# Two more seven-product pairs per half and three DMA-made low parts, in the three projections to the model width

## The chip, the cores and the metric

One core of a Trainium2 chip runs the whole program. The metric is the device time of one execution in microseconds; for one core that is the time of this core. PE is the matrix engine (TensorE), DVE the vector engine (VectorE), ACT the scalar engine (ScalarE), POOL is GpSimd, SP is the engine that issues the loads (SyncE). HBM is the memory outside the core, SBUF the working memory inside it, and PSUM the eight accumulator banks that PE writes.

## The reference

The reference computes two layers of an encoder on 256 positions of width 2048, all in float32. Each layer is a token mixer and a gated feed-forward network (FFN), each followed by a layer norm with a scaled residual:

```python
for i in range(DEPTH):                      # DEPTH = 2
    m = gmlp_mixer(...) if i % 2 == 0 else mla_mixer(...)
    x = layer_norm(ALPHA * x + m, ...)
    f = conv_ffn(x, ...)
    x = layer_norm(ALPHA * x + f, ...)
```

The first mixer ends in `(u * s) @ w_out` with w_out of 6144 x 2048; each FFN ends in `(silu(g) * a) @ w_down` with w_down of 5504 x 2048. These three products, of 48, 43 and 43 row blocks of 128, are the "projections to the model width" that the change touches. Their left operands have 256 rows.

## The kernel before, in words

**Products of split numbers.** PE multiplies numbers of a shortened float32 (float32r). To keep the precision, each operand is cut into a high part (the number rounded to float32r) and a low part (the number minus its high part), and a product is three matmuls: high x high, low x high, high x low (`prod_b`, lines 280 to 286). The left operand is held on chip; the weights come from HBM once and are cut on chip. ACT makes the high part of a chunk of weights (line 104, a copy with rounding), DVE the low one (line 105, a subtraction).

**The feed.** All weights of the program, in the order of their use, are one list of chunks of 128 x 2048 numbers, 1 MB each; `Feed` (lines 66 to 143) loads them on SP's queue (`_load`, line 80 or 85), cuts them (`_split`) and hands them out (`next`). When chunk i is handed out, the cutting of chunks i+1 and i+2 and the loading of two more have been written into the program. All these tiles (raw, high `wh`, low `wl`, and others) share one pool of 22 buffers of 8 KB per partition with the operands that live longer (line 152). A tile takes a buffer over when the last reader of the tile before it is done, so a load can be held up by PE, DVE or ACT. The engines run their own instructions strictly in the order in which they were written.

**A pair of row blocks.** In a projection a chunk holds two consecutive row blocks k, k+1 of the weights for one half of the 2048 columns. The plain way to multiply them with the two blocks of 128 positions is `Banks.eight` (line 337): two position blocks x two column groups of 512 x two k, eight products of 128 x 128 by 128 x 512, 24 matmuls. The other way is `Banks.seven` (line 344), Strassen's scheme in Winograd's form: seven products, 21 matmuls, of sums of the operands. The sums of the weights are made by `Feed._seven` (line 115): DVE adds 1024, 512 and 512 columns (`ts`), then ACT and DVE cut the plain quarters that are needed (`wh`, `wl`, 1536 columns) and the sums (`th`, `tl`, 1536 and 512 columns). The sums of the left operand are made by `combine` (line 206): four DVE operations of 128 x 128, one ACT cast and one DVE subtraction of 128 x 512; they are made once and used in both halves (`Sums.make`, line 396). A seven-product pair takes five buffers of the pool beside its raw chunk. Its four further accumulators are PSUM banks of their own (`OWN`, line 324); after the last such pair of a half `rest` (line 354) adds them up on ACT and DVE and `fold` adds the results to the residual.

**A projection.** `down` (line 405) runs the left half of the columns, then the right half, over the pairs in the order of `halves(n_k)` (line 53): the left half in ascending order, the right half in an order of "quads" of four row blocks. `BACK_SEVEN` (line 63) lists the first row block of the five pairs per half that go by seven products: 4, 10, 18, 24, 32. The last three pairs of the right half are kept back for the start of the layer norm. Left operands are cut quad by quad as they are needed (`quad`, line 384) and dropped after their last use.

The chunk kinds are "seven", "wide" (cut in one piece) and "" (cut in two pieces); `back` (line 174) sets them for the projections.

Of the kernel before, what the change touches and what calls it, by code (L numbers as in the profile page):

```python
# [12 lines left out]
ALU = mybir.AluOpType  # L13
# [36 lines left out]
V_SEVEN = [()] + [(2, 3, 4)] * 5  # L50


def halves(n_k):


    one = [tuple(range(k, min(k + 2, n_k))) for k in range(0, n_k, 2)]
    n = (n_k + 3) // 4
    quads = [n - 1, 1, 2, 0, 4, 3, 6, 8, 5, 7] + list(range(9, n - 1))
    return [one, [u for q in quads for u in one[2 * q : 2 * q + 2]]]

BACK_SEVEN = (4, 10, 18, 24, 32)


class Feed:
# [24 lines left out]
    def _split(self):  # L91
        i = self.split
        cols, kind = self.chunks[i][1:]
        raw = self.raw.pop(i)
        if kind == "seven":
            self.parts[i] = self._seven(i, raw)
            self.split += 1
            return
        hi = self.pool.tile([P, 2048], F32R, tag="big", name=f"wh{i}")
        lo = self.pool.tile([P, 2048], F32R, tag="big", name=f"wl{i}")  # L100
        step = 512 if i == 0 else cols if kind == "wide" and i > 2 else 1024 if cols == 2048 else cols // 2
        for o in range(0, cols, step):
            c = slice(o, o + step)
            self.nc.scalar.copy(hi[:, c], raw[:, c])  # L104
            self.nc.vector.tensor_tensor(lo[:, c], raw[:, c], hi[:, c].bitcast(F32), ALU.subtract)  # L105
            if i == 0 and o == step:
                self.between[1]()
        self.parts[i] = (hi, lo)
        self.split += 1
# [20 lines left out]

    def ahead(self, n_load, n_split):
        while self.split < min(n_split, len(self.chunks)):
            if self.loaded == self.split:
                self._load()
            self._split()
        while self.loaded < min(n_load, len(self.chunks)):
            self._load()
# [9 lines left out]
def trunk(ctx: ExitStack, tc: tile.TileContext, x, xT, gm_in, gm_wout, ffn_up, ffn_dn,  # L147
# [19 lines left out]
    chunks = []  # L167
# [6 lines left out]
    def back(w, n_k):  # L174

        for hf, units in enumerate(halves(n_k)):
            c = slice(hf * 1024, (hf + 1) * 1024)
            for u in units:
                if len(u) == 1:
                    chunks.append((w[u[0], :, c], 1024, "wide"))  # L180
                else:
                    chunks.append((w[u[0] : u[0] + 2, :, c].rearrange("k p c -> p k c"), 2048,
                                   "seven" if u[0] in BACK_SEVEN else "wide"))

    back(gm_wout, NF_GM)
    chunks += [(ffn_up[0, i], 2048, "") for i in range(n_up)]
    back(ffn_dn[0], NF_FF)
    chunks += [(ml_q[i], 2048, "") for i in range(4)]
    chunks += [(ml_kv[i], 3 * KVR, "") for i in range(5)] + [(ml_kv[5, :, 0:KVR], KVR, "")]
    chunks += [(ml_b[i], 2048, "") for i in range(ml_b.shape[0])]  # L190
    chunks += [(ml_out[i], 2048, "") for i in range(ml_out.shape[0])]
    chunks += [(ffn_up[1, i], 2048, "") for i in range(n_up)]
    back(ffn_dn[1], NF_FF)


# [209 lines left out]
    def down(n_k, src, tag, ln, sums, skew=SKEW):  # L405
# [3 lines left out]
        quads = sums.quads  # L409
        late = []  # L410
        for hf, units in enumerate(halves(n_k)):
            n = len(units)
            last = [u for u in units if u[0] in BACK_SEVEN][-1]


            acc = Banks(f"{tag}{hf}", OWN + DIRECT if hf else DIRECT + OWN)
            for i, u in enumerate(units):
                left = n - 1 - i if hf == 1 else n
                for u2 in units[i : i + 3]:
                    sums.quad(u2[0] // 4, n_k)  # L420
                if i + 1 < n and units[i + 1][0] in BACK_SEVEN:
                    sums.make(units[i + 1][0])
# [5 lines left out]
                if left < skew:  # L428
                    late.append((a, *got))
                elif u[0] in BACK_SEVEN:  # L430
                    acc.seven(a, sums.got[u[0]], *got)
# [246 lines left out]
    for gi in range(12):  # L678
        acc = [bank(f"u{gi}_{f}") for f in range(4)]
        for c in range(4):  # L680
            hi, lo = feed.next()
# [5 lines left out]
        if gi == 10:  # L687
            for k in BACK_SEVEN[:2]:
                sums.make(k)
# [17 lines left out]
    def ffn(layer, ln, acc, end, last):  # L707
# [27 lines left out]
        for gi in range(1, 22):  # L735
# [13 lines left out]
            if gi == 20:  # L749
                for k in BACK_SEVEN[:2]:  # L750
                    sums.make(k)
# [66 lines left out]
    for c in range(6):  # L818
        hi, lo = feed.next()
        for j in range(3 if c < 5 else 1):  # L820
            k = 3 * c + j
# [31 lines left out]
    for c in range(2):  # L853
        hi, lo = feed.next()
        for j in range(2):
            k = 2 * c + j
# [107 lines left out]
    for hf in range(2):  # L964
        acc = [[bank(f"vv{hf}_{b}_{f}") for f in range(2)] for b in range(2)]
        for c in range(2):
            hi, lo = feed.next()
            for j in range(2):

                k = 2 * c + j  # L970
# [7 lines left out]
        for b in range(2):  # L978
            for f in range(2):
                c = slice(hf * 1024 + f * 512, hf * 1024 + (f + 1) * 512)  # L980
# [7 lines left out]
    for t in range(3, H + LAG):  # L988
        k = t - LAG
        if k >= 0:  # L990
            if k % 2 == 0:
                hi, lo = feed.next()
            w = slice((k % 2) * 1024, (k % 2) * 1024 + 1024)
# [21 lines left out]
    for c in range(8):  # L1015
        left = 7 - c
        hi, lo = feed.next(splits=2 if left > 5 else 3 if left > 2 else 4, loads=2 if left > 2 else 1)
        for j in range(2):
            k = 2 * c + j
            w = slice(j * 1024, (j + 1) * 1024)  # L1020
# [104 lines left out]
```

## Time and profile before

| what | value |
|---|---|
| time, median of 3 runs | 2501.7 us (2501.2 to 2503.17) |
| the profiled execution | 2504.94 us, its span 2503.2 us |
| granted clock of PE, mean | 0.997 |
| first projection (gMLP), about | 552 to 800 us of the span |
| second (FFN of layer 0), about | 1293 to 1512 us |
| third (FFN of layer 1), about | 2266 to 2490 us |
| read from HBM, written | 476.00 MB, 2.10 MB |

The profile's page gives the busy time of each engine over the span, then the chain of work that ended last, followed back from the last instruction, and groups of equal instructions with count, busy time and mean duration; other views show the same instructions by stretch of time, by line or in order. A row such as `L105 DVE TENSOR_TENSOR wl<-raw,wh` is the instruction of line 105 that writes tile wl from raw and wh; buffer numbers are left out, so one row stands for many chunks. Matmuls are pipelined: the pitch between two is shorter than the duration of one. In the rows of stretches the columns are: stretch, its length, then the busy time and number of instructions of PE, PE's weight loads, DVE, ACT and POOL, then the granted clock, the share of the DMA queues and GB/s.

### The profile page before, as it was taken

How to read it: one execution, taken by the hardware profiler on the slowest of the kernel's cores; microseconds unless marked ns; L12 is line 12 of the kernel's file. 1: busy time of each engine (PE TensorE's matmuls, PEld its weight loads, DVE VectorE, ACT ScalarE, POOL GpSimd, SP SyncE). 2: the span in 40 equal slices, each digit the busy share in tenths (PEclk: the TensorE clock that was granted, in tenths of full speed). 3: DMA queues.
4: the chain of work that ended last, by engine and by line, in shares of the span. 5: the costliest groups of instructions: out<-in, count | busy, mean ns of one | idle time of the engine just before them, and what ended most of it. 6: DMA issues, size and time to landing. Idle time of an engine off the chain costs nothing.

```text
span 2503.2 us, 32484 instructions
## 1 busy us (share of the span) xinstructions
PE 2484.7 (99%) x13066; PEld 2138.5 (85%) x13066; DVE 1840.0 (74%) x2439; ACT 1335.0 (53%) x1763; POOL 2.9 (0%) x17
## 2 busy tenths in 40 slices
PE   9999999999999999999999999999999999999998
PEld 7888888888887888888888888988888888888886
DVE  6887866678787767666778887756686676668796
ACT  6565644445464546545655564565365555546553
POOL 0000000000000000000000000000000000000000
PEclk9999999999999999999999999999999999999999
DMA  7555554556566555555546674444555455555654
GB/s 276 214 190 202 202 177 161 184 192 204 187 207 252 188 182 202 185 180 176 195 156 202 217 269 157 156 143 178 183 205 183 165 206 178 182 180 172 214 203 168
DMA packets 86310, 480.19 MB, mean 192 GB/s; under 512 B 7696, under 2 KB 8336, under 8 KB 46608
## 3 DMA queue, kind: packets, MB, share of 16 engines
q1 hardware_dynamic: 86160, 478.13, 54.2%
q8 instruction: 102, 1.67, 0.3%
q14 instruction: 48, 0.39, 0.0%
HBM read 476.00 MB, written 2.10 MB: 191 GB/s over the span
## 4 chain that ended last, share of the span: by engine, by line
PE 98%; DVE 1%; ACT 0%; DMA 0%; issue 0%; SPq 0%; DVEq 0%; ACTq 0%
PE up L164 36%; PE u L164 11%; PE dn_q L164 9%; PE dn_p L164 6%; PE v_q L164 5%; PE wo_q L164 5%; PE v_p L164 3%; PE mo L164 3%; PE dn_e L164 3%; PE wo_p L164 3%; PE wo_e L164 2%; PE upf L164 2%; PE v_e L164 2%; PE mkv L164 1%; PE qn L164 1%; PE kn L164 1%
## 5 line engine op out<-in xcount | busy, mean ns | idle before, releaser
L105 DVE TENSOR_TENSOR wl<-raw,wh 128x1024 fp32r<-128x1024 f32 (+3 forms) x664 | 929.3, 1424 | 218.7 <-ACT wh L104 161.4
L104 ACT CAST wh<-raw 128x1024 fp32r<-128x1024 f32 (+3 forms) x664 | 786.4, 1215 | 341.1 <-DVE wl L105 125.2
L164 PE MATMUL up<-xhl,wh 128*128 128x512 f32 x2624 | 610.7, 390 | 0.0
L164 PEld LDWEIGHTS up<-xhl,wh 128*128 128x128 f32 x2624 | 487.4, 188 | 97.7
L164 PEld LDWEIGHTS up<-xhl,wl 128*128 128x128 f32 x2624 | 325.8, 192 | 6.4
L164 PE MATMUL up<-xhl,wl 128*128 128x256 f32 x2624 | 328.1, 283 | 0.0
L164 PE MATMUL u<-xhl,wh 128*128 128x512 f32 x768 | 183.8, 393 | 0.3 <-DVE h_u L309 0.2
L164 PEld LDWEIGHTS u<-xhl,wh 128*128 128x128 f32 x768 | 141.3, 188 | 30.8 <-PE s L164 2.1
L112 ACT CAST th<-ts 128x1536 fp32r<-128x1536 f32 x90 | 93.0, 1052 | 113.7 <-DVE ts L119 84.1
L113 DVE TENSOR_TENSOR tl<-ts,th 128x1536 fp32r<-128x1536 f32 x90 | 106.5, 1219 | 13.1 <-ACT th L112 12.2
L164 PEld LDWEIGHTS u<-xhl,wl 128*128 128x128 f32 x768 | 95.6, 192 | 2.0
L164 PE MATMUL u<-xhl,wl 128*128 128x256 f32 x768 | 96.7, 283 | 0.0
L112 ACT CAST wh<-raw 128x1536 fp32r<-128x1536 f32 x45 | 66.7, 1482 | 46.9 <-DMA raw<-in_ffn_dn_dram 13.2
L164 PE MATMUL wo_q<-wh,woa 128*128 128x512 f32 x288 | 88.9, 389 | 0.0
L113 DVE TENSOR_TENSOR wl<-raw,wh 128x1536 fp32r<-128x1536 f32 x45 | 78.8, 1752 | 6.3 <-PE dn_q L164 2.8
L164 PE MATMUL mo<-wh,oT 128*128 128x512 f32 x256 | 82.8, 404 | 0.0
L164 PE MATMUL v_q<-wh,xhl 128*128 128x512 f32 x264 | 82.0, 392 | 0.0
L164 PE MATMUL dn_q<-wh,dn0a 128*128 128x512 f32 x248 | 76.5, 389 | 0.0
L164 PE MATMUL dn_q<-wh,dn1a 128*128 128x512 f32 x248 | 76.3, 389 | 0.0
L309 DVE TENSOR_TENSOR h_0a<-up,lo_0a 128x256 f32<-128x256 f32 x41 | 17.2, 420 | 74.2 <-ACT lo_0a L307 74.1
L309 DVE TENSOR_TENSOR h_1a<-up,lo_1a 128x256 f32<-128x256 f32 x41 | 17.2, 420 | 73.3 <-ACT lo_1a L307 73.3
L164 PEld LDWEIGHTS wo_q<-wh,woa 128*128 128x128 f32 x288 | 54.1, 188 | 11.2
(490 smaller groups left out, 3847.7 us busy)
## 6 DMA issues: line engine op xcount, KB each, us to landing
raw<-in_ffn_up_dram SPq DMA_DIRECT2D x172, 1024.0 KB, 4.7
raw<-in_gm_in_dram SPq DMA_DIRECT2D x93, 1024.0 KB, 4.7
raw<-in_ffn_dn_dram SPq DMA_DIRECT2D x84, 1024.0 KB, 5.3
raw<-in_gm_wout_dram SPq DMA_DIRECT2D x48, 1024.0 KB, 5.3
raw<-in_ml_out_dram SPq DMA_DIRECT2D x16, 1024.0 KB, 4.8
raw<-in_ml_b_dram SPq DMA_DIRECT2D x14, 1024.0 KB, 4.8
raw<-in_ml_kv_dram SPq DMA_DIRECT2D x5, 864.0 KB, 4.4
lng<-in_ln_rows_dram SPq DMA_DIRECT2D x4, 1024.0 KB, 8.6
```

The source lines that it names most:

```text
L104: self.nc.scalar.copy(hi[:, c], raw[:, c])
L105: self.nc.vector.tensor_tensor(lo[:, c], raw[:, c], hi[:, c].bitcast(F32), ALU.subtract)
L112: self.nc.scalar.copy(hi, raw)
L113: self.nc.vector.tensor_tensor(lo, raw, hi.bitcast(F32), ALU.subtract)
L164: nc.tensor.matmul(o, l, r, start=start, stop=stop, skip_group_check=True)
L309: nc.vector.tensor_tensor(h, acc[:, 0:S], lo, ALU.add)
```

## The change

In each of the three projections it does three things.

- Seven row-block pairs per half, not five, go by seven products: those that begin at 4, 10, 16, 22, 28, 34 and 38.
- Three chunks per half get the kind "low", by their place in the half: places 6, 12 and 18 of the left, 6, 8 and 13 of the right. ACT first writes minus the rounded weights into the low tile (a multiplication by -1), POOL then issues a DMA that adds the same weights from HBM to that tile, and ACT makes the high part. DVE has no part in it. Such a chunk is cut one chunk earlier than others (`ahead`).
- The right half takes the quads in another order, three of them with their two pairs exchanged.

```diff
+BACK_SEVEN = (4, 10, 16, 22, 28, 34, 38)
+BACK_LOW = ((6, 12, 18), (6, 8, 13))
 def halves(n_k):
...
-    quads = [n - 1, 1, 2, 0, 4, 3, 6, 8, 5, 7] + list(range(9, n - 1))
-    return [one, [u for q in quads for u in one[2 * q : 2 * q + 2]]]
-BACK_SEVEN = (4, 10, 18, 24, 32)
+    two = []
+    for q in [n - 1, 1, 2, 4, 5, 0, 7, 8, 9, 3, 6] + list(range(10, n - 1)):
+        two += one[2 * q : 2 * q + 2][:: -1 if q in (4, 8, 9) else 1]
+    return [one, two]
...
         hi = self.pool.tile([P, 2048], F32R, tag="big", name=f"wh{i}")
         lo = self.pool.tile([P, 2048], F32R, tag="big", name=f"wl{i}")
+        if kind == "low":
+            self.nc.scalar.mul(lo, raw, -1.0)
+            self.nc.gpsimd.dma_start(lo.rearrange("p (k c) -> p k c", k=2), self.chunks[i][0], accum_op=ALU.add)
+            self.nc.scalar.copy(hi, raw)
+            self.parts[i] = (hi, lo)
+            self.split += 1
+            return
...
             self._split()
+        if self.split < len(self.chunks) and self.chunks[self.split][2] == "low":
+            if self.loaded == self.split:
+                self._load()
+            self._split()
         while self.loaded < min(n_load, len(self.chunks)):
             self._load()
...
-            for u in units:
+            for i, u in enumerate(units):
...
-                                   "seven" if u[0] in BACK_SEVEN else "wide"))
+                    kind = "seven" if u[0] in BACK_SEVEN else "low" if i in BACK_LOW[hf] else "wide"
+                    chunks.append((w[u[0] : u[0] + 2, :, c].rearrange("k p c -> p k c"), 2048, kind))
```

In the right half the pairs by place are now: 0 and 1 the last quad, 2 seven (row block 4), 3 and 4 plain, 5 seven (10), 6 low (18), 7 seven (16), 8 low (20), 9 seven (22), 10 and 11 plain, 12 seven (28), 13 low (30), 14 seven (34), 15 plain, 16 seven (38), and plain ones from there.

More of the change, by code (lines that the diff above doesn't have):

```diff
@@ L181, in back @@
                 else:
-                    chunks.append((w[u[0] : u[0] + 2, :, c].rearrange("k p c -> p k c"), 2048,
-                                   "seven" if u[0] in BACK_SEVEN else "wide"))
+                    kind = "seven" if u[0] in BACK_SEVEN else "low" if i in BACK_LOW[hf] else "wide"
+                    chunks.append((w[u[0] : u[0] + 2, :, c].rearrange("k p c -> p k c"), 2048, kind))
     back(gm_wout, NF_GM)
```

## The prediction, on record before the run

> **What bounds the kernel now.** First the head of the page and the shares of the chain that ended last, then the waits of PE alone:
>
> ```profile
> span 2503.2 us, 32484 instructions
> ## 1 busy us (share of the span) xinstructions
> PE 2484.7 (99%) x13066; PEld 2138.5 (85%) x13066; DVE 1840.0 (74%) x2439; ACT 1335.0 (53%) x1763; POOL 2.9 (0%) x17
> PE 98%; DVE 1%; ACT 0%; DMA 0%; issue 0%; SPq 0%; DVEq 0%; ACTq 0%
> ```
>
> ```profile
> PE upf L164 <- DVE xhl L574: 2.2, 1, 2.2
> PE v_p L164 <- ACT wh L104: 1.7, 1, 1.7
> PE mq L164 <- DVE xhl L574: 1.5, 1, 1.5
> ```
>
> PE is the bound, and it waits hardly anywhere; its longest waits are at the changes of stage, none in a projection. So a matmul taken out of a projection is worth its full pitch, and every microsecond by which weights come late is lost in full. From the chain in order of time comes the pitch, from the stretches of time the load on the other engines in one projection (first layer's FFN, four quarters):
>
> ```profile
> 1502.18 5.44 PE dn_q L164 x24
> ```
>
> ```profile
> 1293.00:1349.00 56.00, 56.00 (x248) 46.37 (x247) 51.46 (x54) 33.92 (x31) 0.31 (x2) 1.00 0.58 188
> 1349.00:1405.00 56.00, 56.00 (x248) 46.38 (x247) 42.69 (x35) 28.83 (x23) 0.00 (x0) 1.00 0.62 202
> 1405.00:1458.00 53.00, 53.00 (x235) 43.92 (x234) 49.55 (x43) 32.38 (x25) 0.00 (x0) 1.00 0.63 207
> 1458.00:1512.00 54.00, 54.00 (x240) 44.70 (x240) 41.78 (x35) 29.57 (x23) 0.00 (x0) 1.00 0.73 270
> ```
>
> 24 matmuls take 5.44 us, 0.2267 us each. DVE (third of the busy columns) is at 51.46 of 56 us in the first quarter, 92%, and PE still never waits; ACT (fourth) stays near 60%.
>
> **The change part by part.** *Removed from PE.* A pair by eight products is 24 matmuls (5.44 us), by seven 21 (4.76 us). Two more pairs per half, two halves, three projections make 12 pairs, 36 matmuls, 36 x 0.2267 = **8.16 us** less, all of it on the path.
>
> *Added to DVE and ACT.* Durations by shape:
>
> ```profile
> L105 DVE TENSOR_TENSOR wl<-raw,wh 128x2048 fp32r<-128x2048 f32 x132 | 301.5, 2289 | 88.4 <-ACT wh L104 74.7 <-issue 9.7 <-PE wo_q L164 2.4
> L104 ACT CAST wh<-raw 128x2048 fp32r<-128x2048 f32 x132 | 251.9, 1912 | 103.4 <-DMA raw<-in_ffn_dn_dram 31.3 <-DMA raw<-in_gm_wout_dram 19.3 <-DVE tl L113 12.4
> L113 DVE TENSOR_TENSOR tl<-ts,th 128x1536 fp32r<-128x1536 f32 x45 | 78.9, 1753 | 6.8 <-ACT th L112 6.0
> L113 DVE TENSOR_TENSOR wl<-raw,wh 128x1536 fp32r<-128x1536 f32 x45 | 78.8, 1752 | 6.3 <-PE dn_q L164 2.8 <-PE v_q L164 2.6 <-PE v_p L164 0.9
> L112 ACT CAST th<-ts 128x1536 fp32r<-128x1536 f32 x45 | 66.9, 1486 | 96.9 <-DVE ts L119 67.3 <-PE v_q L164 12.3 <-PE dn_q L164 6.5
> L112 ACT CAST wh<-raw 128x1536 fp32r<-128x1536 f32 x45 | 66.7, 1482 | 46.9 <-DMA raw<-in_ffn_dn_dram 13.2 <-PE v_q L164 8.2 <-PE wo_q L164 7.6
> L119 DVE TENSOR_TENSOR ts<-ts,raw 128x512 f32<-128x512 f32 x90 | 61.8, 687 | 1.4
> L119 DVE TENSOR_TENSOR ts<-raw 128x1024 f32<-128x1024 f32 x45 | 54.9, 1220 | 8.4 <-DMA raw<-in_ffn_dn_dram 4.2 <-PE u L164 1.6 <-PE wo_q L164 1.5
> L113 DVE TENSOR_TENSOR tl<-ts,th 128x512 fp32r<-128x512 f32 x45 | 30.8, 684 | 6.2 <-ACT th L112 6.2
> L112 ACT CAST th<-ts 128x512 fp32r<-128x512 f32 x45 | 27.8, 617 | 16.8 <-DVE ts L119 16.8
> ```
>
> ```profile
> L211 DVE TENSOR_TENSOR xsdn<-act x10: 280/284/293, 896.3 to 2285.3; 128x128 f32<-128x128 f32 x10
> L217 DVE TENSOR_TENSOR dn0xc<-xsdn,dn0xc x5: 684/684/693, 1286.3 to 1373.2; 128x512 fp32r<-128x512 f32 x5
> ```
>
> A seven-product pair costs DVE 1.22 + 2 x 0.69 + 1.75 + 1.75 + 0.68 = 6.78 us, a plain one 2.29: 4.49 more, four times per projection, 18.0. Two more sums of the left operand (`combine`: four of 0.28 and one of 0.68, 1.8 each) add 3.6. Six chunks with kind "low" have no subtraction: -13.7. Net +7.9 on DVE's 185.5 us of the four quarters, of 219 - 2.7 us: 193.4 of 216.3, 89%. ACT gains 4 x 1.67 + 6 x 1.91 + 1.2 = 19.4 us on 124.7, 67%. Both fit beside PE, and 92% in the first quarter caused no wait, so I cost this work **at nothing**; if that cover fails where DVE's work bunches (a seventh pair, its sums and the next half's first pair stand close together), I estimate up to 2 us per projection. The other order of the second half moves no work of its own; no quad is split more often. The last seven-product pair of a half is nearer to the half's end (`rest` at place 19, not 16), but two units follow it, 8.2 us, for four additions of 0.69: nothing.
>
> *The accumulating DMA.* A low part is made by ACT (`-round(raw)`, 1.91) and then by a 1 MB DMA from POOL that adds the raw weights from HBM. POOL is empty (2.9 us busy), so nothing queues behind its wait but the next such DMA. The trace has no accumulating DMA. Nearest rows, the medians of issue to landing of 1 MB, and the queues' rate while one load ran:
>
> ```profile
> raw<-in_ffn_dn_dram SPq DMA_DIRECT2D x84, 1024.0 KB, 5.3
> ...
> lnb<-in_ln_rows_dram SPq DMA_DIRECT2D x4, 1024.0 KB, 10.5
> ```
>
> ```profile
> DMA packets 191, 0.77 MB, mean 383 GB/s; under 512 B 4, under 2 KB 4, under 8 KB 191
> ...
> q1 hardware_dynamic: 191, 0.77, 99.7%
> ```
>
> One load keeps all queues busy (99.7%) at 383 GB/s, so 1.05 MB hold them 2.7 us. The addition reads a second stream, the 1 MB in SBUF. Below: a plain load, 5.3 us; above: 10.5, the 1 MB row that lands last behind another. I take a plain load and a second pass of the queues, 5.3 + 2.7 = **8.0 us**, between them. Worth less than nothing it cannot be: before, that MB was not moved at all, and what it saves, DVE's time, is counted above.
>
> *How much time it has.* In the second half the places are: 2 seven, 3 and 4 plain, 5 seven, 6 low, 7 seven, 8 low, 9 seven. Let T be the start of unit 2. PE then starts unit 3 at 4.76, 4 at 10.20, 5 at 15.64, 6 at 20.40, 7 at 25.84, 8 at 30.60, and asks for a plain unit's low part two matmuls later, 0.45. In the profile before, the same place 5 was made so (PE's row is T, the SP row the issue of 5's load):
>
> ```profile
> 1414.30 0.39 PE L164 MATMUL dn_p<-wh,dn0a 128*128 128x512 f32 x1
> ```
>
> ```profile
> 1414.49 0.37 SPq L80 DMA_DIRECT2D raw<-in_ffn_dn_dram  x1
> ```
>
> ```profile
> 1419.96 1.49 ACT L112 CAST wh<-raw 128x1536 fp32r<-128x1536 f32 x1 [1.00 <-DMA raw<-in_ffn_dn_dram]
> 1423.42 1.49 ACT L112 CAST th<-ts 128x1536 fp32r<-128x1536 f32 x1 [1.97 <-DVE ts L119]
> ```
>
> The load went at T+0.2, the large cast of the sums ended at T+10.6. The change puts more tiles into the same 22 buffers (five per seven-product pair, a fourth for the sums, hi and lo of a low chunk a unit earlier). By the program's order of buffers the load of place 5 then takes the buffer of wh of unit 2, free at T+4.1: landed 9.4, wh 9.4 to 10.9, DVE's two adds, behind the plain low part of 4 (load from T, 5.3, cast 1.91, subtraction 2.29: 9.5), to 11.4, th 11.4 to 12.9. Only behind this th does ACT's order have the -1 copy of place 6: 12.9 to 14.8; POOL issues at 14.9. PE asks at 20.85. That leaves **5.95 us**; with 8.0 the DMA is 2.05 late.
>
> Place 7's load takes wh of unit 4, free at 15.64, and runs beside that DMA, so it lands at 15.64 + 5.3 + 2.7 (the queues shared) = 23.6; without the sharing 20.9. Its adds (1.91, wh beside them) and th (1.49) end at 27.0, the copy for place 8 to 28.9, POOL at 29.0, landed 37.0. PE, 2.05 late, asks at 31.05 + 2.05 = 33.1: 3.9 late. Together **5.95 us** per projection. Place 13 has time: its pair 12 is not short of buffers, and by the same walk its DMA has 8.8 us. In the first half a low stands behind a seven too, but there the loads aren't late. Place 5 of an FFN projection, its large th and the start of its pair on PE:
>
> ```profile
> 1313.45 1.49 ACT L112 CAST th<-ts 128x1536 fp32r<-128x1536 f32 x1 [4.23 <-DVE ts L119]
> ```
>
> ```profile
> 1319.10 0.39 PE L164 MATMUL dn_p<-wh,dn0a 128*128 128x512 f32 x1
> ```
>
> th ends 4.15 us ahead of the pair, the -1 copy 2.25 ahead, POOL starts 2.15 ahead, and place 6 is asked for 4.76 + 0.45 behind: 7.35 us, 0.65 late, in two projections. Places 12 and 18 I give place 13's 8.8: in time.
>
> *What a stall costs beside itself.* The stretches around PE's 2.2 us wait (PEclk is third from the end):
>
> ```profile
> 807.00:810.00 3.00, 0.80 (x7) 0.48 (x5) 3.00 (x5) 0.58 (x1) 0.00 (x0) 1.00 0.67 205
> 810.00:815.00 5.00, 5.00 (x17) 3.95 (x18) 3.66 (x6) 0.19 (x1) 0.00 (x0) 0.66 0.24 102
> ...
> 1522.00:1528.00 6.00, 5.39 (x25) 4.33 (x26) 5.74 (x10) 0.59 (x1) 0.00 (x0) 1.00 0.33 133
> ```
>
> PE had 0.80 busy us in 3; then the granted clock was 0.66 over 5 us, 1.7 us lost. Behind the wait of 1.5 us (mq, last row) it stayed 1.00. So the 3.9 us stall costs 1.7 more, the one of 2.05 nothing (bounds: 0 and 1.7 for each).
>
> **Sum.** 3 x (5.95 + 1.7) + 2 x 0.65 - 8.16 = +16.1 us. The profiled execution took 2504.94 us, its span 2503.2; it would take 2521.0. The median shown is 3.2 lower, 2501.7, and becomes **2517.8**.
>
> *A page on that DMA.* The Trainium skill, "Collectives: The Full Stack", The bandwidth ceiling, says that an add in the DMA path halves the rate because it reads two sources, and "DMA: Bandwidth & Descriptors", Anatomy of one DMA, gives 2.0 us plus bytes at 436 GB/s for a DMA from GpSimd. An estimate from both is 2.0 + 2 x 2.4 = 6.8 us, and by it the stalls at places 6 and 8 would be 0.85 and 3.9 us, the kernel +11, 2513. No run here shows it yet.
>
> **The rivals.** *R1, faster:* the low parts land in time, and the 8.16 us stay. Place: units 6 and 8 of the second half. It decides when the stalls of one projection sum to less than 1.05 us (2.7 saved, less 1.7, a third of 5 us): the DMA under 5.5 us and the load of place 7 undelayed, or ACT reaching the copies 3 us sooner than I walked. For it: the projections before have no wait, and ACT, free a third of its time, could be ahead of my walk. Against: even a plain load of 5.3 leaves unit 8 with 4.65 us (POOL at 26.4, asked at 31.05). Time 2501.7 - 8.2 = 2493.5. Chance 0.28.
> *R2, even:* a DMA of 5.3 us and the load of place 7 delayed by half, 1.35: place 8 is 26.4 + 1.35 + 5.3 - 31.05 = 2.0 late, and with 0.7 of bunching the 2.7 saved per projection are gone: 2501.7. Chance 0.12.
> *Forecast:* DMAs of 7 to 9 us. At 7 (place 6 late by 1.05, place 8 by 3.9 more, its slow clock, nothing in the first half) +12, at 9 (3.05, 3.9, one slow clock more, 1.65 twice) +26; with the load of place 7 delayed less, 5 under the first: 2508 to 2528. Chance 0.43.
> *R3, dearer:* 10.5 us as lnb's row. Place 6 is 4.55 late, place 8 3.9 more, both with a slow clock (3.4), places 12, 13 and 18 1.7 each, the bunching 2: 18.95 per projection, place 6 of the first half 3.15 in two: 63.2 - 8.2 = +55, 2557. Chance 0.17.
> That the change doesn't do what it says is out: 36 matmuls and 18 subtractions fewer are in the program's order.
>
> **How the numbers follow.** This kernel's measurement tells some 0.2%, 5 us, from no change. Faster is R1, 0.28; same R2, 0.12; slower the rest, 0.60. The range leaves out R3's upper half and the little beyond R1's end: 2493 to 2550; the forecast's own is 2508 to 2528.
>
> **What would show it.** Right: the waits of PE name POOL's DMA (wl) or its landing, twice per second half, some 2 and 4 us, with a granted clock of half for a few us behind the longer; the DMA row of wl reads 7 to 9 us; a seven-product pair still takes 4.76. Wrong: that row under 5.5 us and no wait of PE in the projections (R1), waits at every low place (R3), or waits of PE for tl or wl from DVE, which would mean that DVE, counted at nothing, is the bound.

## The result and the profile after

The changed kernel takes 2620.8 us (median of 4 runs, 2619.74 to 2624.73) against 2502.4 for the kernel before on the same chip: ratio 1.0476, 95% interval 1.0463 to 1.0488. It is 118 us slower; the prediction said 16, and its range ended at 2550. Direction right, size far off.

First the head of the page after (line numbers are 12 to 17 higher than before), its rows of queues, the shares of the chain that ended last and the rows of DMA issues (size, median us from issue to landing):

```profile
span 2620.0 us, 32665 instructions
## 1 busy us (share of the span) xinstructions
PE 2514.4 (96%) x13030; PEld 2149.3 (82%) x13030; DVE 1858.7 (71%) x2511; ACT 1386.1 (53%) x1811; POOL 24.6 (1%) x35
...
q1 hardware_dynamic: 86160, 478.13, 51.3%
q0 software_dynamic: 4896, 18.88, 3.9%
...
PE 79%; DMA 8%; DVE 7%; issue 4%; ACT 1%; SPq 0%; DVEq 0%; POOLq 0%; ACTq 0%
...
raw<-in_ffn_dn_dram SPq DMA_DIRECT2D x84, 1024.0 KB, 5.8
...
wl<-in_ffn_dn_dram POOLq DMA_DIRECT2D x12, 1024.0 KB, 10.9
wl<-in_gm_wout_dram POOLq DMA_DIRECT2D x6, 1024.0 KB, 10.2
```

PE does the 36 matmuls less (13066 to 13030), yet is 30 us longer busy: its matmuls run longer while the clock is low. DMA is now 8% of the chain, where it was 0%. The 18 accumulating DMAs land 10 to 11 us after their issue, not 8.0, and the plain loads have gone from 5.3 to 5.8 us in the FFNs' projections and from 5.3 to 6.2 in the first. The waits of PE:

```profile
PE dn_q L181 <- DMA wl<-in_ffn_dn_dram: 45.5, 11, 7.5
PE wo_q L181 <- DMA wl<-in_gm_wout_dram: 21.4, 5, 8.1
PE lnt L587 <- DVE res L576: 12.4, 8, 3.4
```

16 of the 18 low parts are waited for, 66.9 us in all. The third row is new too: at the changes of stage PE waits for the layer norm. What such a stall looks like, and what the clock does behind it, at the third low part of the left half of the first projection (columns as in the rows of stretches of the kernel before):

```profile
640.00:650.00 10.00, 8.64 (x39) 6.82 (x37) 4.10 (x4) 5.57 (x4) 1.20 (x1) 1.00 0.70 169
650.00:654.00 4.00, 0.00 (x0) 0.00 (x0) 3.93 (x5) 3.07 (x4) 0.00 (x0) 0.63 1.04 274
654.00:664.00 10.00, 7.96 (x24) 6.38 (x25) 3.15 (x4) 1.27 (x3) 0.00 (x0) 0.64 0.37 142
```

POOL issued at 641.92 (its one instruction in the first row). PE does nothing from 648.6 to 656.0, the queues are full (1.04), and the granted clock is at half from 651 to 661.

**Where the 117 us of the two profiles went**, counted by the starts of the matmuls. From first to last matmul the three projections take 27.1, 33.6 and 32.6 us longer, 93.4 in all: some 75 of standing still and 24 of half clock, a few us of smaller gaps, less 8.2 for the matmuls that are gone. From the last matmul of a projection to the first of the next it is 9.2 and 12.2 us longer, behind the last matmul 3.5; the first projection starts 1.6 sooner. PE's gaps at the low parts (what is above the pitch of 0.2267 us), 69.8 us in all:

| place | first projection | second | third |
|---|---|---|---|
| left 6 | 1.6 | 3.9 | 3.0 |
| left 12 | 1.9 | 2.5 | 2.0 |
| left 18 | 7.6 | 7.7 | 7.2 |
| right 6 | 8.4 | 6.4 | 5.9 |
| right 8 | 0 | 0.7 | 0.1 |
| right 13 | 2.9 | 3.8 | 4.2 |

**The boundary.** The scheduler that writes the program put PE's matmuls of the kept-back units in another order. Before, it was bank by bank, so the first residual pieces were ready long before the projection's end (the last matmul there ended at 807.1):

```profile
794.26 0.69 DVE L544 TENSOR_TENSOR res<-res,wo_q 128x512 f32<-128x512 f32 x1 [4.03 <-PE wo_q L164]
798.34 0.69 DVE L544 TENSOR_TENSOR res<-res,wo_p 128x512 f32<-128x512 f32 x1 [2.66 <-PE wo_p L164]
```

Now the four banks are interleaved, and the same two pieces come 6.8 and 5.0 us ahead of the end (832.7), not 12.8 and 8.8; behind it PE is busy 6 of 14 us, at a clock of 0.58:

```profile
825.89 0.69 DVE L561 TENSOR_TENSOR res<-res,wo_q 128x512 f32<-128x512 f32 x1 [8.65 <-PE wo_q L181]
827.71 0.69 DVE L561 TENSOR_TENSOR res<-res,wo_p 128x512 f32<-128x512 f32 x1 [1.13 <-PE wo_p L181]
```

```profile
833.00:847.00 14.00, 6.00 (x18) 4.11 (x19) 14.00 (x22) 5.79 (x8) 0.00 (x0) 0.58 0.21 75
```

### The profile page after: what moved, and what is told of

Read it like the earlier page. It is cut to its first block, busy times and chain, and to the rows that moved or that the text cites. A ratio compares the mean times of both kernels' runs of the same rounds, so it can differ in the third digit from the quotient of the medians.

```text
span 2620.0 us, 32665 instructions
## 1 busy us (share of the span) xinstructions
PE 2514.4 (96%) x13030; PEld 2149.3 (82%) x13030; DVE 1858.7 (71%) x2511; ACT 1386.1 (53%) x1811; POOL 24.6 (1%) x35
## 4 chain that ended last, share of the span: by engine, by line
PE 79%; DMA 8%; DVE 7%; issue 4%; ACT 1%; SPq 0%; DVEq 0%; POOLq 0%; ACTq 0%
PE up L181 34%; PE u L181 10%; DMA wl<-in_ffn_dn_dram 5%; PE v_q L181 4%; PE dn_q L181 3%; PE mo L181 3%; PE v_p L181 3%; PE wo_q L181 3%; PE dn_p L181 3%; DVE wl L117 2%; DMA wl<-in_gm_wout_dram 2%; PE upf L181 2%; PE v_e L181 2%; PE wo_p L181 2%; PE dn_e L181 1%
## 5 line engine op out<-in xcount | busy, mean ns | idle before, releaser
L117 DVE TENSOR_TENSOR wl<-raw,wh 128x1024 fp32r<-128x1024 f32 (+3 forms) x634 | 861.1, 1384 | 195.3 <-ACT wh L116 152.5
L116 ACT CAST wh<-raw 128x1024 fp32r<-128x1024 f32 (+3 forms) x634 | 728.2, 1181 | 312.2 <-DVE wl L117 121.2
L124 ACT CAST th<-ts 128x1536 fp32r<-128x1536 f32 x114 | 118.3, 1048 | 126.6 <-DVE ts L131 84.2
L125 DVE TENSOR_TENSOR tl<-ts,th 128x1536 fp32r<-128x1536 f32 x114 | 136.8, 1221 | 26.4 <-ACT th L124 23.8
L124 ACT CAST wh<-raw 128x1536 fp32r<-128x1536 f32 x57 | 84.4, 1480 | 101.6 <-DMA raw<-in_ffn_dn_dram 61.7
L131 DVE TENSOR_TENSOR ts<-raw 128x1024 f32<-128x1024 f32 x57 | 69.6, 1221 | 54.5 <-DMA raw<-in_ffn_dn_dram 40.0
L125 DVE TENSOR_TENSOR wl<-raw,wh 128x1536 fp32r<-128x1536 f32 x57 | 99.9, 1752 | 3.5 <-PE v_q L181 2.5
L181 PE MATMUL wo_q<-wh,woa 128*128 128x512 f32 x256 | 80.6, 394 | 0.3 <-DVE woa L408 0.3
L131 DVE TENSOR_TENSOR ts<-ts,raw 128x512 f32<-128x512 f32 x114 | 78.5, 688 | 1.9
L181 PE MATMUL wo_q<-wl,woa 128*128 128x512 f32 x128 | 51.6, 403 | 21.5 <-DMA wl<-in_gm_wout_dram 21.4
## 6 DMA issues: line engine op xcount, KB each, us to landing
wl<-in_gm_wout_dram POOLq DMA_DIRECT2D x6, 1024.0 KB, 10.2
```

The source lines that it names most:

```text
L124: self.nc.scalar.copy(hi, raw)
L125: self.nc.vector.tensor_tensor(lo, raw, hi.bitcast(F32), ALU.subtract)
L131: add = lambda o, a, b: self.nc.vector.tensor_tensor(o, a, b, ALU.add)
L181: nc.tensor.matmul(o, l, r, start=start, stop=stop, skip_group_check=True)
```

## The experiments

Theory A: the accumulating DMAs are late and PE waits for them. Rival B: the two more seven-product pairs make everything late. Theory C: PE's other order at the boundaries costs its own share. Later two more: Q, the queues that the addition holds make the loads late; H, the buffer that it holds does.

### One half of the change at a time

`sevens_alone`, the changed kernel without low chunks:

```diff
-BACK_LOW = ((6, 12, 18), (6, 8, 13))
+BACK_LOW = ((), ())
```

> The seven seven-product pairs and the new order stay, the low parts are all made by DVE again. Theory A (the accumulating DMAs are late by themselves): the waits of PE for wl from a DMA go (66.9 us of waits, and the slow clock behind them), the 36 matmuls stay away (-8.2), and what is left of a loss is at the boundaries, because PE's order of the last three units is still not quite bank by bank: 2492 to 2502. Theory B (the two more seven-product pairs, with their five buffers each and 4.5 us of DVE work, make everything late and the low chunks only show it): the projections still stall, now for wl or tl from DVE and for loads: 2530 or more.

2519.6 us, ratio 1.0064 (1.0051 to 1.0078), the number of neither theory: no stall of note in the projections, so B falls as the main cause, but it is no gain either. PE's longest wait is the boundary's:

```profile
PE lnt L587 <- DVE res L576: 10.4, 6, 2.8
```

From the last matmul of a projection to the first of the next it was 7.5 and 11 us longer than before, behind the last matmul 2.7.

`lows_alone`, the pairs and order of before with three low chunks per half (shown against the kernel before; the code that makes a low chunk is the changed kernel's):

```diff
 BACK_SEVEN = (4, 10, 18, 24, 32)
+BACK_LOW = ((6, 13, 18), (6, 8, 16))
```

> The five seven-product pairs and the order of before, plus three accumulating DMAs per half, at places 6, 13, 18 and 6, 8, 16. Theory A: each of 18 DMAs takes 9 to 14 us from issue to landing and PE waits 2 to 8 us for most, with the clock at half behind the longer waits: 2570 to 2620. Theory B: with five seven-product pairs there is slack, the DMAs land in time or nearly: 2500 to 2525.

2634.5 us, ratio 1.0523 (1.0508 to 1.0537): the low chunks alone cost 132 us, more than theory A's range. Their rows of issue to landing and of PE's waits:

```profile
wl<-in_ffn_dn_dram POOLq DMA_DIRECT2D x12, 1024.0 KB, 12.9
wl<-in_gm_wout_dram POOLq DMA_DIRECT2D x6, 1024.0 KB, 14.0
```

```profile
PE dn_q L181 <- DMA wl<-in_ffn_dn_dram: 54.3, 12, 6.9
PE wo_q L181 <- DMA wl<-in_gm_wout_dram: 28.4, 5, 7.5
```

### PE's order at the boundaries

`bank_order`, the changed kernel with the matmuls of the kept-back units bound to the order of the program:

```diff
-            mm(acc[f][:, :w], xh, hi[:, o : o + w], first, False)
+            keep(mm(acc[f][:, :w], xh, hi[:, o : o + w], first, False))
...
+                           False, i == len(late) - 1 and j == len(a[b]) - 1, tc.keep_in_program_order)
```

> The changed kernel, with the matmuls of the three kept-back units bound to the order of the program (bank by bank), nothing else. Theory C (PE's other order there makes the residual's pieces late): the wait for lnt of 8 us goes, and with it some 13 us at the two boundaries and 2 to 3 us at the end: 2603 to 2608. Rival (the pieces are late because the weights of these units are late): PE then waits inside the banks, and the time stays within 2616 to 2622.

2611.5 us, ratio 1.0430 (1.0416 to 1.0444): 9.3 us less, so C is real, though smaller than the 13 to 18 us that it expected: the first transposes now stand in PE's queue ahead of the last bank, and PE waits there.

```profile
PE lnt L587 <- DVE res L576: 8.9, 2, 4.4
```

`sevens_bank_order`, both edits, no DMA:

> The seven pairs and the new order without accumulating DMAs, and the matmuls of the kept-back units bound to the program's order. With the sevens alone the two boundaries were 7.5 and 11 us longer than before and the end 2.7 us, the projections themselves 0.4 to 1.3 us above what 12 matmuls less make each. Theory C (all of that is PE's order of the last units): the boundaries return to those of before and the 8.2 us stay saved but for some 3: 2496 to 2501, faster than before. Rival (the low parts of the last units are late from DVE whatever PE's order): 2512 to 2520.

2510.1 us, ratio 1.0030 (1.0019 to 1.0041), above theory C's 2496 to 2501: PE's order is not all of it. The same row, 8.9 us in two waits, is in its profile, with 3.4 us of half clock behind each, and two waits of 2.4 us together in the last projection, also with 3.4 us of half clock behind them. From here on this kernel is the base.

`sevens_before_end` and `sevens_end_mended` give PE the order of before: the last bank's first 12 matmuls, then the first transposes.

```diff
         end(1, fs[0])
+        end(1, fs[1], (0, 1))
         ln.put(0, 0)
         ln.piece(1, fs[0], acc[1][fs[0]])
-        end(1, fs[1])
+        end(1, fs[1], (2,))
```

> Seven pairs, new order, no accumulating DMA, and at the boundaries PE's order of the kernel before (the last bank's first twelve matmuls ahead of the first transposes, the transposes in their order). In bank order alone PE stood 4.4 us twice at the first transposes, with 3 us of slow clock behind them. Theory C: these 12 us go and what the 36 matmuls save remains but for some 4 us in the projections: 2497 to 2500. Rival (DVE, with two more pairs, is late with the residual and the wait moves on): 2505 or more.

2506.0 us, ratio 1.0014 (1.0005 to 1.0023), but this kernel leaves out one of four kept-back units of the last projection, 24 matmuls. With them:

> Seven pairs, new order, no accumulating DMA, PE's order at the boundaries as in the kernel before; the run sevens_before_end with the 24 matmuls (5.4 us) that it left out of the last projection. Theory: 2506.0 + 5.4 = 2511.4, so 8 to 10 us slower than before: the two more pairs then give back at the ends of the stages, where DVE makes the residual's pieces and the next stage's low parts, what they save. Rival (what was left out carried a stall as well): up to 2514.

2511.4 us, ratio 1.0032 (1.0020 to 1.0045): no better than bank order. The wait has moved on:

```profile
PE lnt L588 <- DVE res L577: 3.4, 2, 1.7
PE upf L181 <- DVE xhl L592: 3.3, 1, 3.3
PE mq L181 <- DVE xhl L592: 3.3, 1, 3.3
```

All of them wait for DVE, which makes the residual's pieces, the layer norm and the next stage's low parts there. `six_pairs` has one pair more, not two:

```diff
-BACK_SEVEN = (4, 10, 16, 22, 28, 34, 38)
+BACK_SEVEN = (4, 10, 16, 22, 28, 34)
...
-    for q in [n - 1, 1, 2, 4, 5, 0, 7, 8, 9, 3, 6] + list(range(10, n - 1)):
+    for q in [n - 1, 1, 2, 0, 4, 5, 3, 7, 8, 6] + list(range(9, n - 1)):
```

> Six pairs per half (4, 10, 16, 22, 28, 34) in an order of quads nearer to that of before, no accumulating DMA, PE's order at the boundaries as in the kernel before: 18 matmuls less, 4.1 us. If the two pairs' loss of 16 us at the stages' ends comes from DVE's work for the last pairs: half of it or less here, 2499 to 2505, at best some 3 us under before. If it comes from binding PE's order there: 2508 or more.

2503.2 us, ratio 1.0004 (0.9995 to 1.0013): even. Of 8.2 us saved by two pairs none is left, and 7 us more are lost; of 4.1 saved by one, nothing is left. So one pair loses some 5 us where two lose 15.3, as it was expected if DVE's work for the last pairs is the cost; but the order of the quads is another one too, so the cause is not shown by this run alone. No version here beats the kernel before.

### The DMA by itself, and what makes it slow

`dma_by_itself` runs six transfers one behind the other after the end of the base:

> The kernel without accumulating DMAs, and behind its end six transfers one after the other, each from the landing of the one before: 1 MB by SP, 1 MB plain by POOL, 1 MB added by POOL, 0.5 MB added by POOL, then the plain and the added one each with a load of SP beside it. The prediction's term (a plain load and a second pass of the queues): 5.3, about 5.3, 8.0, 5 and with a load beside 8 and 10.7. Theory A1 (two sources, twice the queue time, and the loads beside it make up the rest of the 10 to 14 us seen in the kernel): 7 to 8.5 us for the added MB alone, 10 to 11 with one load. Rival (the addition is slow in itself): 10 us or more with nothing beside it.

```diff
+    for i, (kind, load) in enumerate([("sp", 0), ("plain", 0), ("add", 0), ("half", 0), ("plain", 1), ("add", 1)]):
+        t, l = slot([P, D], f"{kind}{i}", F32 if kind == "sp" else F32R), slot([P, D], f"beside{i}")
+        nc.scalar.mul(t, prev, -1.0)
...
+        prev = t if kind == "sp" else t.bitcast(F32)
```

The queues and the issues in the stretch of 5.6 us with SP's load alone, of 6.0 us with the plain copy by POOL alone, of 9.3 us with the added MB alone, and of 12.9 us with the added MB and a load by SP beside it:

```profile
q1 hardware_dynamic: 272, 1.05, 52.9%
issues: line engine op xcount, KB each, median us to landing
sp<-in_ffn_dn_dram SPq DMA_DIRECT2D x1, 1024.0 KB, 5.1
```

```profile
q0 software_dynamic: 272, 1.05, 53.9%
issues: line engine op xcount, KB each, median us to landing
plain<-in_ffn_dn_dram POOLq DMA_DIRECT2D x1, 1024.0 KB, 5.6
```

```profile
q0 software_dynamic: 272, 1.05, 61.4%
issues: line engine op xcount, KB each, median us to landing
add<-in_ffn_dn_dram POOLq DMA_DIRECT2D x1, 1024.0 KB, 8.9
```

```profile
beside<-in_ffn_dn_dram SPq DMA_DIRECT2D x1, 1024.0 KB, 6.4
add<-in_ffn_dn_dram POOLq DMA_DIRECT2D x1, 1024.0 KB, 11.4
```

Half the addition landed in 5.6 us, the plain copy beside a load in 8.5. The addition holds all queues for 0.614 x 9.3 = 5.7 us, the plain copy for 0.539 x 6.0 = 3.2, SP's load for 0.529 x 5.6 = 3.0: the addition costs 1.8 times the queue time of the copy. In the changed kernel 3.9% of 2620 us for 18 of them is the same 5.7 us each. Its 8.9 us alone and 11.4 beside a load are somewhat above theory A1's 7 to 8.5 and 10 to 11, and under the 10 alone of the rival (the addition is slow in itself): of the 3.3 us between addition and copy 2.5 are queue time, and what the rest is, these runs don't show.

`plain_copy`, the changed kernel without the addition (the low tile then holds the whole weights, so the result is another one):

```diff
-            self.nc.gpsimd.dma_start(lo.rearrange("p (k c) -> p k c", k=2), self.chunks[i][0], accum_op=ALU.add)
+            self.nc.gpsimd.dma_start(lo.rearrange("p (k c) -> p k c", k=2), self.chunks[i][0])
```

> The changed kernel with the addition taken out of the DMA: POOL issues a plain copy of 1 MB to the low tile at the same place, so the low part of these chunks holds the whole weights (the output is another one). Theory A1 (the addition reads two sources, so it holds the queues twice as long): the copies land in 6 to 8 us, not 9 to 14, the queue time of that queue halves to some 2%, and the waits of PE fall by more than half: 2540 to 2580. Theory A2 (what is slow is the way through POOL's queue, whatever it carries): the copies take 9 to 14 us too and the time stays at 2610 to 2622.

2564.9 us, ratio 1.0247 (1.0233 to 1.0261), 55.9 less than the changed kernel. A1 holds, A2 falls:

```profile
q0 software_dynamic: 4896, 18.88, 2.2%
```

```profile
wl<-in_ffn_dn_dram POOLq DMA_DIRECT2D x12, 1024.0 KB, 7.8
wl<-in_gm_wout_dram POOLq DMA_DIRECT2D x6, 1024.0 KB, 7.0
```

### Does it cost only because PE waits for it?

`unread`, in bank order: the DMA adds into a tile of its own, DVE makes the low part.

```diff
-            self.nc.scalar.mul(lo, raw, -1.0)
-            self.nc.gpsimd.dma_start(lo.rearrange("p (k c) -> p k c", k=2), self.chunks[i][0], accum_op=ALU.add)
+            un = self.pool.tile([P, 2048], F32R, tag="big", name=f"un{i}")
+            self.nc.scalar.mul(un, raw, -1.0)
+            self.nc.gpsimd.dma_start(un.rearrange("p (k c) -> p k c", k=2), self.chunks[i][0], accum_op=ALU.add)
             self.nc.scalar.copy(hi, raw)
+            self.nc.vector.tensor_tensor(lo, raw, hi.bitcast(F32), ALU.subtract)
```

> The changed kernel in bank order, with the accumulating DMA going to a tile of its own that nobody reads; DVE makes the low part as it does for other chunks. The DMAs hold the queues as before, but PE doesn't wait for them. Theory A (the loss is PE waiting for a late landing): 2500 to 2515. Rival Q (the loss is that the DMA holds the queues 5.7 us per MB and makes the loads behind it late): the waits go over to loads and to what is made of them, 2560 or more.

2574.2 us, ratio 1.0287 (1.0273 to 1.0301): 64 us above the base although nobody waits for the DMA. Theory A alone falls. Now ACT stands at the casts of weights whose load is late; its waits in the base (first fence) and here:

```profile
ACT wh L124 <- DMA raw<-in_ffn_dn_dram: 15.9, 9, 2.9
```

```profile
ACT wh L126 <- DMA raw<-in_ffn_dn_dram: 52.7, 10, 9.9
```

Part of that is the buffer: SP holds back loads until the added tile's buffer comes free, 47.8 us in six waits:

```profile
SPq L84 <- DMA un<-in_ffn_dn_dram: 29.2, 4, 9.7
SPq L84 <- DMA un<-in_gm_wout_dram: 18.6, 2, 11.3
```

`one_unit_earlier`, the changed kernel in bank order with the low chunks cut a unit sooner (`_split` passes over what is cut already):

```diff
-        if self.split < len(self.chunks) and self.chunks[self.split][2] == "low":
-            if self.loaded == self.split:
-                self._load()
-            self._split()
+        for j in range(self.split, min(self.split + LEAD, len(self.chunks))):
+            if self.chunks[j][2] == "low" and j not in self.parts:
+                while self.loaded <= j:
+                    self._load()
+                at, self.split = self.split, j
+                self._split()
+                self.split = at
```

with `LEAD = 2`.

> The changed kernel in bank order, with a low chunk cut two units ahead of the others' turn, not one, so some 5 us sooner. Theory A: stalls of 2 to 8 us lose up to 5 each, and the slow clock with them: 2515 to 2550. Rival (two more buffers held 5 us longer make the loads late, or the copy by ACT waits for its load in front of ACT's other work): 2590 or more.

2610.9 us, ratio 1.0427 (1.0413 to 1.0442), against 2611.5: nothing. What the earlier start gives, the loads lose: PE's waits for low parts fall from 65.9 to 43.0 us, but ACT, which asks for its chunks sooner, waits 179 us for loads of the projections, not 120, and PE 12 us for casts of the seven-product pairs, for which it waited nowhere in bank order.

### Queue and buffer taken apart

`unread_plain`, a plain copy into the tile that nobody reads:

```diff
-            self.nc.gpsimd.dma_start(un.rearrange("p (k c) -> p k c", k=2), self.chunks[i][0], accum_op=ALU.add)
+            self.nc.gpsimd.dma_start(un.rearrange("p (k c) -> p k c", k=2), self.chunks[i][0])
```

> The tile that nobody reads, filled by a plain 1 MB copy from POOL in place of the addition: 3.2 us of all queues (measured by itself), not 5.7. Theory Q, with what is above 5.4 us of queue time per unit of PE lost: 3.0 + 3.2 is 0.8 above, 3.0 + 5.7 is 3.3 above, so a quarter of the loss of 64 us: 2525 to 2535. Theory H: the buffer is held 7 to 8 us, not 11, and the loss is two thirds: 2550 to 2560.

2543.5 us, ratio 1.0161 (1.0147 to 1.0176): between the two. `held_only`, the tile held by five small additions:

```diff
-            self.nc.gpsimd.dma_start(un.rearrange("p (k c) -> p k c", k=2), self.chunks[i][0], accum_op=ALU.add)
+            for _ in range(5):
+                self.nc.gpsimd.dma_start(un[:, 0:16], self.chunks[i][0][:, 0, 0:16], accum_op=ALU.add)
```

> As the kernel whose added tile nobody reads (2574 us), but in place of the 1 MB five additions of 8 KB into that tile, each waiting for the one before: the tile's buffer is held about as long, some 10 us, and the queues are left free. Theory Q (the queues are the cost: an addition takes 5.7 us of all of them beside a load of 3 us per 5.4 us of PE): 2510 to 2525. Theory H (the cost is the buffer that comes free late, so that a later load starts late): 2560 to 2575. In between both have a share, read off by the distance from 2510.

2627.6 us, ratio 1.0489 (1.0472 to 1.0506), above what either theory expected. Beside loads each small DMA took some 4 us, so the tile was held some 20 us, twice as long as meant. `held_two` has two of them:

> The tile that nobody reads is held by two additions of 8 KB one after the other, not five: with 4 to 5 us for each beside loads that is some 10 us, as long as by the added MB (11.4), and the queues stay free. Theory H (the buffer that comes free late): 2555 to 2575, near the 2574 with the added MB. Theory Q (the queues): 2510 to 2520.

2529.8 us, ratio 1.0108 (1.0094 to 1.0121), between the two theories: 19.7 us above the base with the tile held some 8 us and the queues all but free. From here to 20 us of holding it is 98 us more, so a tile held long is dear. The landing of its small DMAs and SP's waits for the tile:

```profile
DMA to landing us min/median/max: 2.2/3.9/7.7
```

```profile
SPq L84 <- DMA un<-in_ffn_dn_dram: 17.0, 4, 5.6
SPq L84 <- DMA un<-in_gm_wout_dram: 10.4, 2, 5.3
```

`queue_plain` and `queue_add` have no tile for the DMA: the weights go to a scratch tensor in HBM when a low chunk has landed, which POOL learns by copying one column of it (shown: `queue_add`; the other leaves out `accum_op`).

```diff
+            self.keep(self.nc.gpsimd.tensor_copy(self.mark, raw[:, 0:1]))
+            self.keep(self.nc.gpsimd.dma_start(un, self.chunks[i][0], accum_op=ALU.add))
```

> No tile is held and none is read: when a low chunk has landed, POOL copies the same 1 MB of weights from HBM to a scratch tensor in HBM, and DVE makes the low part. The queues are held by some 3 us per copy (as the plain copy into SBUF) or a little more. Theory H: 2508 to 2515. Theory Q: 2520 to 2535.

2533.7 us, ratio 1.0122 (1.0108 to 1.0136).

> As the run before, with the addition: the 1 MB is added to the scratch tensor in HBM, some 6 us of all queues or more, and no buffer is held. Theory H: 2508 to 2520. Theory Q: 2550 to 2580.

2551.1 us, ratio 1.0191 (1.0176 to 1.0207), with this queue row:

```profile
q0 software_dynamic: 4896, 18.88, 4.3%
```

Above the base of 2510.1 `queue_add` is 41.1 us, `held_two` 19.7, 60.8 by their sum, and `unread`, with both, 64.1. But neither number is a clean price. These kernels share two things with the changed one beside the DMA: ACT makes one pass more over each low chunk (1.91 us), and that chunk is cut a unit sooner. No run has these two alone, and PE's waits say that they, or something else that is common, have a part. In the base PE has one wait of note in the projections of the FFNs (first fence); with the tile held (`held_two`, second) and with the queues used (`queue_plain`, third) it waits for the same tiles and for about as long, in the second and third projection at the same units too:

```profile
PE dn_q L181 <- DVE dn1a L408: 1.9, 1, 1.9
```

```profile
PE dn_q L184 <- DVE dn1a L411: 3.9, 3, 1.9
PE dn_q L184 <- DVE wl L120: 3.7, 5, 1.7
PE dn_q L184 <- DVE dn0a L411: 2.5, 2, 1.3
```

```profile
PE dn_q L186 <- DVE dn1a L414: 4.6, 3, 1.9
...
PE dn_q L186 <- DVE wl L122: 3.3, 3, 1.7
PE dn_q L186 <- DVE dn0a L414: 2.7, 2, 1.4
```

So a common part, at most the 19.7 of `held_two`, may be in both numbers. Free of it are the differences between kernels that have it alike: the addition in place of the copy costs 17.4 us through the queues alone (`queue_plain` to `queue_add`), and 30.6 where it also holds a tile longer (`unread_plain` to `unread`). The queues have a share of their own, then, and long holding has one; how large each is in the changed kernel is not shown. Nor are the two quite apart: POOL's copy took 15 us at two of the 18 low chunks and kept their loaded buffer so long (SP waited 11.7 us for it), and the addition into HBM held the queues slightly longer than that in the kernel (4.3% against 3.9% of about the same span).

`one_low`, bank order with one low chunk per half at the places that the prediction called in time:

```diff
-BACK_LOW = ((6, 12, 18), (6, 8, 13))
+BACK_LOW = ((12,), (13,))
```

> The changed kernel in bank order with one accumulating DMA per half, place 12 of the left and 13 of the right, the places that the prediction called in time (8.8 us). If it was right there: 2510 as with none. With 9 to 11 us per addition each is 1 to 2 us late: 2515 to 2525. If each of the 18 additions costs the same 5.6 us ((2611.5 - 2510.1) / 18): 2544.

2541.2 us, ratio 1.0149 (1.0132 to 1.0165): 31.1 us for six, 5.2 each, near the 5.6 each of the eighteen, and not in time: PE waits at all six.

```profile
PE dn_q L181 <- DMA wl<-in_ffn_dn_dram: 12.2, 4, 5.0
...
PE wo_q L181 <- DMA wl<-in_gm_wout_dram: 6.2, 2, 4.4
```

### The steps from before to after

| kernel | us | step |
|---|---|---|
| before (measured beside the next) | 2502.9 | |
| seven pairs, new order, bank order | 2510.1 | +7.1: 8.2 saved, 15.3 lost |
| and 18 additions that nobody reads | 2574.2 | +64.1: queues, buffers, ACT's pass, the earlier cut |
| and PE reads them, DVE doesn't subtract | 2611.5 | +37.4: waiting for the landing |
| and the scheduler's own order at the boundaries (the change) | 2620.8 | +9.3 |

The kernel of the second step has a buffer more per low chunk than the change itself, beside the two that both hold a unit sooner; so the line between the second and the third step is not sharp. Their sum, 101.5, is.

## Why the prediction was wrong

- **"36 x 0.2267 = 8.16 us less": right.** The matmuls are gone, at the same pitch where nothing stands.
- **"5.3 + 2.7 = 8.0 us" for the DMA: the term that was mis-sized.** It took the addition as a second pass of 2.7 us; it holds the queues 5.7 us, and alone it lands in 8.9. (The 2.7 was read from 2 us in which not one load ran but two, issued at 1411.77 and 1414.49; by itself a load holds the queues 3.0 us.) And it was sized alone, though it always runs beside loads: 11.4 us with one, 9.0 to 14.2 in the kernel, median 10.7. The rule that the prediction took from the Trainium skill, "Collectives: The Full Stack", The bandwidth ceiling (an add reads two sources and halves the rate, said there of collectives), is borne out by the queue time, 1.8 times; the estimate worked out from it and from "DMA: Bandwidth & Descriptors", Anatomy of one DMA, 6.8 us, is under the 8.9 measured.
- **"That leaves 5.95 us", "7.35 us", "in time": windows of the right size, read against the wrong duration.** Landing time less gap gives left place 6 7.2 to 8.3 us (predicted 7.35), place 12 about 8.3 (8.8), place 18 6.5 (8.8), right place 6 3.9 in the first projection and 7.0 in the others (5.95), place 13 6.7 to 6.9 (8.8). With 9 to 14 us none but place 8 is in time, and that one only because PE had just stood 6 to 8 us at place 6. There, where the prediction put its longer stall, 3.9 us, PE lost at most 0.7.
- **What the DMA does to others was counted once, at place 7, for 2.7 us. This is the step that failed most.** A unit of PE is 5.44 us, its load holds the queues 3.0; an addition of 5.7 more is 3.3 above what fits. The loads behind it come late, and so does every load that waits for a buffer; 18 x 3.3 is some 59 us. The runs give 41 us for 18 additions into HBM and 64 for 18 into a tile that nobody reads, ACT's pass and the earlier cut included. So even the rival with the right duration, R3 with 10.5 us, came out at 2557.
- **DVE and ACT "at nothing", up to 2 us per projection: failed, in part at another place.** In the projections of the changed kernel PE waited 3.6 us for DVE and ACT, all three together. But without low chunks the two more pairs save 8.2 us and lose 15.3: by the profile of `sevens_bank_order` some 6 us at the two boundaries, 6 in the last projection (waits for low parts that DVE makes, and the half clock behind them) and 3 in the others. ACT's pass over the low chunks and their earlier cut, also counted at nothing, may have cost up to the 19.7 us of `held_two`.
- **PE's order at the boundary wasn't in the prediction.** "The other order of the second half moves no work of its own" looked at the program's order; the scheduler wrote another one, 9.3 us. The description of the kernel has the same fault: the engines do not run their instructions in the order in which they were written, but in the one that the scheduler gives them, and at these boundaries the two differ.
- **"1.7 us" of slow clock per long stall: right in kind.** There are 14 stretches at half clock, 111 us in all, 11 of them (72 us) in the projections, not one in each. In the changed kernel's projections gaps of up to 2.0 us had none behind them, of 2.5 to 3.9 mostly 3.4 us (one of 2.9 had none), of 4.2 to 8.4 us 6.8 to 10.2.
- **"Waits of PE name POOL's DMA": right**, though at five places of a projection (all but place 8) rather than at two or three.

What stays open: why the low chunks cost 132 us with five pairs and 101 with seven (the landing takes a median of 13.5 us there, 10.6 here), how the loss divides among the queues, the buffers, ACT's pass and the earlier cut, and how much of the boundary's loss is DVE's work and how much its order.

## What to carry to other kernels

Price a new DMA in the kernel's own queue time per step, not only by when it lands: here a step of 5.44 us had room for 2.4 us more of the queues and got 5.7, and a third to a half of the loss, 41 to 64 of 118 us, comes even when nobody waits for the DMA. Count the pool buffer that a slow transfer keeps as a wait of the loads behind it. Where a scheduler writes the engine's order, compare that order at the ends of the stages before trusting that an edit in the middle leaves them alone, and ask whether the relieved engine was on the path at all: in the projections DVE was not, so what it was spared could pay for nothing.

## What the runs showed of the hardware

- An accumulating 1 MB DMA from POOL holds all queues 5.7 us and lands alone in 8.9 us; a plain one 3.2 and 5.6; half the addition lands in 5.6. With a load beside it the added MB takes 11.4, and the load 6.4 in place of 5.1.
- A DMA of 8 KB from POOL, beside loads of 1 MB, took 2.2 to 7.7 us, median 3.9; a chain of five kept a tile some 20 us. That it queues behind the large ones is likely, but not shown.
- The half clock came in stretches of about 3.4 us or multiples of it, but for those at the end of a run. A gap of 2.1 us between matmuls was enough to start one (`sevens_bank_order`, 2475 us), while 2.9 us (the changed kernel, 772 us) and 3.6 us (`six_pairs`, 1516 us) started none.
